# A down projection in seven products: sums of weight quarters kept in T, product order, and adds on POOL

## The chip, the cores and the metric

The kernel runs on one core of one Trainium2 chip. The core's engines work side by side: TensorE (PE in the profile, its weight loads PEld), VectorE (DVE), ScalarE (ACT), GpSimd (POOL) and SyncE (SP), which here only starts transfers. Each has its own instruction queue and meets the others through semaphores; transfers run on 16 DMA engines that all queues share. The metric is the device time of one execution in microseconds (us), as the median of several runs.

## The reference

One decoder layer on 512 tokens of width 1024, all in float32: two mixers (a state-space scan and a forgetting attention) with their projections, then a gated MLP with a causal convolution. The change touches the last matrix product of the MLP alone:

```
h = x @ w_up; h = causal_depthwise_conv(h, conv_w, conv_b)
gate, val = jnp.split(h, 2, axis=-1)
return (jax.nn.silu(gate) * val) @ w_down        # (512 x 2816) @ (2816 x 1024)
x = x + conv_gated_mlp(hf, ...)
```

## The kernel before, in words

**Precision.** TensorE takes operands in a shortened float format (fp32r). Each float32 operand is therefore split into a high part (a cast, on ScalarE) and a low part (the rest, a subtraction on VectorE), and each product is three matmuls: high by high, high by low, low by high (`mm3`, lines 110 to 112). For a weight unit that is `split_unit` (lines 726 and 727), for a left operand `split_into` (lines 756 and 757).

**Seven products.** The hidden activations (512 tokens by 2816) are cut in two token halves and two halves of the inner dimension, the weights w_down in two inner halves and two column halves: B11, B12, B21, B22. The block product is made in Strassen's manner with seven products of quarters in place of eight (Winograd's form): sums of activation quarters (`S1` to `S4`, and `a11`, `a12`, `a22`) by sums of weight quarters. The activation sums are made while the up projection runs (`sums`, lines 778 to 787, on POOL). The weight sums are made in the seven products, in the tiles T.

**A product.** A weight quarter is six units: five of two blocks of 128 x 512 (512 KB) and one of one block (256 KB). For each unit a product splits it into `wh` and `wl`, and runs 12 matmuls per block, two token blocks of 128 by three passes by two; in all 66 matmuls of 512 columns for the 11 blocks. Of `wh` and `wl` there are three buffers each, which the units use in turn; a unit's split can start when TensorE is done with the unit three back. The last two units of a product are taken together, sorted by token block. The result in PSUM (tiles X, Y, Z) is added to or subtracted from the residual tile `x2` on VectorE (line 874), and a finished block is stored (line 876). Products that share a result accumulate in one PSUM tile: Y in three of them, Z in two.

**Where the weights come from.** A plain quarter is loaded into a staging buffer `wraw` (`load_unit`, line 715; five buffers, SP's queue) and split from there. A sum is made in T: `fresh` (line 806) loads a quarter into T on SP's queue, and `gather` (line 809) adds another one by an accumulating transfer, on POOL's queue. T is a running sum. `next_sum(n, u)` is called after unit u of product n has been split; it may then be overwritten, with the sum that a later product wants. Before the change:

| product | left by weights | weights from | after its split, T becomes |
|---|---|---|---|
| 0 | a11 by B11 | wraw (three units split ahead, in `ready`) | B11 loaded, B12 accumulated |
| 1 | a12 by B21 | wraw | |
| 2 | S1 by T = B11 + B12 | T | B22 accumulated |
| 3 | S2 by T = B11 + B12 + B22 | T | B21 accumulated |
| 4 | a22 by T = all four | T | B22 loaded, B12 accumulated |
| 5 | S3 by T = B22 + B12 | T | |
| 6 | S4 by B22 | wraw | |

**Memory.** T's pool is opened after the up projection's pool (`pu`) is closed and takes its place in SBUF; a T tile may be written when the tiles that lay on its bytes are done with.

**Order.** The text gives every instruction's dependences and its place in program order. A planner (the tile framework's, line 950) sets the order of the instructions of each engine when the kernel is built: it moves ahead what it reckons to be ready. On the chip each queue then runs strictly in that order. So the left operand's split for a product three places on runs as soon as the buffer of a finished product's left operand is free, that is, where products meet.

Of the kernel before, what the change touches and what calls it, by code (L numbers as in the profile page):

```python
# [55 lines left out]
def tile_hybrid_layer(  # L56
# [20 lines left out]
    act, dve, pool, pe = nc.scalar, nc.vector, nc.gpsimd, nc.tensor  # L77
# [10 lines left out]
    def raw(ap):  # L88
        return ap.bitcast(F32)
# [18 lines left out]
    def mm3(o, ah, al, bh, bl, start, stop, grouped=True):  # L108
        kw = {} if grouped else {"skip_group_check": True}
        pe.matmul(o, ah, bh, start=start, stop=False, **kw)  # L110
        pe.matmul(o, ah, bl, start=False, stop=False, **kw)  # L111
        pe.matmul(o, al, bh, start=False, stop=stop, **kw)  # L112

    def bank(name="g"):
        return pg.tile([P, 512], F32, tag="g", name=name)

    def mbank(name="m"):
        return pm.tile([P, 512], F32, tag="m", name=name)
# [574 lines left out]
    def operand(slot=None):  # L693
        if slot is None:
            hl_ = [pb.tile([P, NH, HT], F32R, tag=t, name=t, bufs=2) for t in ("oh", "ol")]
            return hl_[0], hl_[1]
        pair_ = [pxt.tile([P, NK, SEQ], F32R, tag=t, name="o" + t) for t in ("xh", "xl")]
        return tuple(
            t.rearrange("p a b -> p (a b)")[:, 0 : NH * HT].rearrange("p (a b) -> p a b", b=HT) for t in pair_
        )  # L700
# [3 lines left out]
    S1, S2, S3, S4 = [pb.tile([P, NH, HT], F32, tag="S%d" % n, name="sum%d" % n) for n in (1, 2, 3, 4)]  # L704
    r2 = pb.tile([P, NTB], F32, tag="r2", name="r2")
    ss = pb.tile([P, NTB], F32, tag="ss", name="ss")
    UNITS = [(k, min(k + 2, NH)) for k in range(0, NH, 2)]
    B11, B12, B21, B22 = 0, 1, 2, 3

    def part(q, u):  # L710
        return wdown[q, :, UNITS[u][0] * 512 : UNITS[u][1] * 512]

    def load_unit(q, u):
        rw = wp.tile([P, 1024], F32, tag="wraw", name="wraw", bufs=5)
        nc.sync.dma_start(rw[:, 0 : (UNITS[u][1] - UNITS[u][0]) * 512], part(q, u))
        return rw
# [3 lines left out]
    def split_unit(u, src):  # L720
        n = (UNITS[u][1] - UNITS[u][0]) * 512
        where = pb if turn[0] % 3 == 2 else wp
        turn[0] += 1
        h = where.tile([P, 1024], F32R, tag="wh", name="wh")
        l = where.tile([P, 1024], F32R, tag="wl", name="wl")
        act.copy(h[:, :n], src[:, :n])  # L726
        dve.tensor_tensor(out=l[:, :n], in0=src[:, :n], in1=raw(h[:, :n]), op=ALU.subtract)  # L727
        return h, l
# [26 lines left out]
    def split_into(o, src, lo, hi):  # L755
        act.copy(o[0][:, lo:hi, :], src[:, lo:hi, :])
        dve.tensor_sub(o[1][:, lo:hi, :], src[:, lo:hi, :], raw(o[0][:, lo:hi, :]))
# [40 lines left out]
    ready = [split_unit(u, load_unit(B11, u)) for u in range(3)]  # L798
# [4 lines left out]
    T = [pt_.tile([P, 512 * (b - a)], F32, tag="T%d" % a, name="T%d" % a) for a, b in UNITS]  # L803

    def fresh(q, u):
        nc.sync.dma_start(T[u], part(q, u))

    def gather(q, u):
        nc.gpsimd.dma_start(T[u], part(q, u), accum_op=ALU.add)

    Y, Z, X1, X2 = (
        [mbank("Y") for _ in range(2)], [mbank("Z") for _ in range(2)], [bank("X") for _ in range(2)], None
    )
    ADD, SUB = ALU.add, ALU.subtract
    PRODUCTS = (
        (B11, None, Y, True, ((0, 0, ADD, False),)),
        (B21, None, X1, True, ((0, 0, ADD, True),)),
        (None, S1, Z, True, ((2, 512, ADD, False),)),
        (None, S2, Y, False, ((0, 512, SUB, False),)),
        (None, a22, X2, True, ((2, 0, ADD, False),)),  # L820
        (None, S3, Y, False, ((2, 0, ADD, True), (2, 512, SUB, True))),
        (B22, S4, Z, False, ((0, 512, ADD, True),)),
    )

    def next_sum(n, u):
        if n == 0:
            fresh(B11, u)
            gather(B12, u)
        elif n in (2, 3):
            gather(B22 if n == 2 else B21, u)  # L830
        elif n == 4:
            fresh(B22, u)
            gather(B12, u)

    ops = [a11, a12]
    for n, (quarter, _, tiles, start, adds) in enumerate(PRODUCTS):
        nxt = PRODUCTS[n + 1][1] if n + 1 < len(PRODUCTS) else None
        if nxt is not None:
            ops.append(operand(1 if n % 3 == 1 else None))
        tiles = [bank("X") for _ in range(2)] if tiles is None else tiles  # L840
        lhs = ops[n]
        final = n == len(PRODUCTS) - 1
        held = []
        for u, (lo, hi) in enumerate(UNITS):
            if n == 0 and u < len(ready):
                h, l = ready[u]
            else:
                h, l = split_unit(u, T[u] if quarter is None else load_unit(quarter, u))
            next_sum(n, u)
            if nxt is not None and u in (1, 2, 3):  # L850
                split_into(ops[n + 1], nxt, 4 * (u - 1), min(4 * u, NH))
            held.append((lo, hi, h, l))
            if u == len(UNITS) - 2:
                continue
            todo = [(k, i, b) for b in held for k in range(b[0], b[1]) for i in range(2)]
            held = []
            if u == len(UNITS) - 1:
                todo.sort(key=lambda t: t[1])
            for k, i, (lo_, _, h_, l_) in todo:
                c = slice((k - lo_) * 512, (k - lo_ + 1) * 512)  # L860
                s = slice(i * P, (i + 1) * P)
                mm3(
                    tiles[i], lhs[0][:, k, s], lhs[1][:, k, s], h_[:, c], l_[:, c], start and k == 0, k == NH - 1,
                    grouped=False,
                )
                if k == NH - 1:
                    for row, col, op, done in adds:
                        tb = row + i
                        cuts = 2 if final and i == 1 else 1
                        w = 512 // cuts  # L870
                        for cut in range(cuts):
                            c = slice(cut * w, (cut + 1) * w)
                            oc = slice(col + cut * w, col + (cut + 1) * w)
                            dve.tensor_tensor(out=x2[:, tb, oc], in0=x2[:, tb, oc], in1=tiles[i][:, c], op=op)
                            if done:
                                nc.sync.dma_start(out[tb * P : (tb + 1) * P, oc], x2[:, tb, oc])
# [77 lines left out]
```

## Time and profile before

| | |
|---|---|
| median of three runs | 845.64 us (845.4 to 849.22) |
| the profiled execution's own time | 845.59 us |
| its span in the trace | 843.8 us |
| TensorE matmuls, busy | 810.0 us (96%), 4590 |
| VectorE, ScalarE, POOL, busy | 630.9, 434.6, 291.4 us |
| plain transfers (q1) | 89.31 MB, 32.3% of 16 DMA engines |
| accumulating transfers (q0) | 11.54 MB, 7.0% |
| mean granted TensorE clock | 0.998 |

How to read it: a line such as `L727 DVE TENSOR_TENSOR wl<-T,wh 128x1024 ... x20` is a group of instructions: line of the kernel, engine, operation, output and inputs by their names in the program (buffer numbers left out), shape, count. "Idle before" is how long the engine stood before them, and the arrow names what ended that. A row of a timeline starts with the start and the duration in us. A row of stretches has, after its bounds and length, each engine's busy time with its instructions in the order PE, PEld, DVE, ACT, POOL, then the granted clock, the DMA engines' busy share and GB/s. A row of DMA queues has packets, MB and the time of its packets as a share of 16 engines over the window. A row of waits reads: who waited, for whom, us in total, times, longest.

### The profile page before, as it was taken

The page shows a single profiled execution, that of the slowest core. Times are in us where ns is not written, and L with a number is a line of the kernel's source. Part 1 is how long each engine was busy: PE and PEld are TensorE (multiplying, and loading weights), DVE is VectorE, ACT ScalarE, POOL GpSimd, SP SyncE. Part 2 cuts the span into 40 slices and gives each one's busy share as a digit, 9 for nine tenths or more (in the row PEclk, how much of TensorE's full clock was granted, in tenths as well). Part 3 has the DMA queues.
Part 4 walks back from the last instruction along what each step waited for, and adds up shares of the span by engine and source line. Part 5 has one row for each costly group of instructions (what it writes and reads, how often), then busy time and mean ns, then how long its engine had stood idle before and what let it go on. Part 6 is the DMA issues. An engine that isn't in the chain of part 4 may idle for free.

```text
span 843.8 us, 12403 instructions
## 1 busy us (share of the span) xinstructions
PE 810.0 (96%) x4590; PEld 696.6 (83%) x4590; DVE 630.9 (75%) x999; ACT 434.6 (52%) x830; POOL 291.4 (35%) x281
## 2 busy tenths in 40 slices
PE   6999989899989999999999999999999999998987
PEld 4888879779989898798898888888888888875766
DVE  7696998775779788997988767666666667875644
ACT  5456546443567675684575364444444444654432
POOL 3125253375445445135133413333333331332210
PEclk9999999999999999999999999999999999999999
DMA  8424322431442332333331222322222333599972
GB/s 313 164 76 130 100 101 76 133 105 50 140 123 86 104 101 92 96 112 107 95 101 51 95 81 100 99 99 89 91 97 100 100 100 109 160 304 240 241 169 88
DMA packets 32285, 101.63 MB, mean 120 GB/s; under 512 B 4129, under 2 KB 4961, under 8 KB 32225
## 3 DMA queue, kind: packets, MB, share of 16 engines
q1 hardware_dynamic: 28768, 89.31, 32.3%
q0 software_dynamic: 3456, 11.54, 7.0%
q8 instruction: 36, 0.59, 0.3%
q14 instruction: 25, 0.20, 0.1%
HBM read 94.44 MB, written 2.20 MB: 115 GB/s over the span
## 4 chain that ended last, share of the span: by engine, by line
PE 67%; DVE 13%; issue 7%; DMA 6%; POOL 3%; ACT 3%; SPq 0%; DVEq 0%; POOLq 0%; ACTq 0%
PE up L112 9%; PE up L110 9%; PE up L111 9%; DMA T<-in_wdown_dram 4%; PE pq L111 4%; PE pq L112 4%; PE pq L110 4%; PE po L112 3%; PE po L111 3%; PE po L110 3%; DVE xs L351 2%; PE o L580 1%; PE pT L566 1%; POOL ms L122 1%; PE Y L111 1%
## 5 line engine op out<-in xcount | busy, mean ns | idle before, releaser
L104 ACT CAST wh<-wraw 128x1024 fp32r<-128x1024 f32 x103 | 108.4, 1053 | 135.5 <-PE up L111 72.1
L110 PE MATMUL pq<-wh,xh 128*128 128x256 f32 x512 | 146.3, 288 | 0.0
L112 PE MATMUL pq<-wh,xl 128*128 128x256 f32 x512 | 146.2, 286 | 0.0
L111 PE MATMUL pq<-wl,xh 128*128 128x256 f32 x512 | 145.3, 284 | 0.6 <-DVE wl L105 0.6
L112 PE MATMUL up<-hh,wl 128*128 128x512 f32 (+1 forms) x368 | 140.2, 381 | 0.2 <-DVE wl L105 0.2
L111 PE MATMUL up<-hl,wh 128*128 128x512 f32 (+1 forms) x368 | 139.9, 380 | 0.0
L110 PE MATMUL up<-hh,wh 128*128 128x512 f32 (+1 forms) x368 | 139.8, 380 | 0.0
L105 POOL TENSOR_TENSOR wl<-wraw,wh 128x1024 fp32r<-128x1024 f32 x31 | 75.3, 2427 | 107.7 <-ACT wh L104 98.6
L105 DVE TENSOR_TENSOR wl<-wraw,wh 128x1024 fp32r<-128x1024 f32 x72 | 90.3, 1254 | 20.0 <-ACT wh L104 19.9
L111 PEld LDWEIGHTS pq<-wl,xh 128*128 128x128 f32 x512 | 97.8, 191 | 2.1 <-DVE wl L105 1.1
L110 PEld LDWEIGHTS pq<-wh,xh 128*128 128x128 f32 x512 | 97.5, 191 | 1.9 <-issue 1.2
L112 PEld LDWEIGHTS pq<-wh,xl 128*128 128x128 f32 x512 | 97.8, 191 | 0.7 <-issue 0.5
L112 PEld LDWEIGHTS up<-hh,wl 128*128 128x128 f32 x368 | 69.2, 188 | 13.8 <-DVE wl L105 0.4
L111 PEld LDWEIGHTS up<-hl,wh 128*128 128x128 f32 x368 | 69.2, 188 | 13.1
L110 PEld LDWEIGHTS up<-hh,wh 128*128 128x128 f32 x368 | 69.1, 188 | 13.1 <-issue 0.2
L765 DVE TENSOR_TENSOR up<-up,R 128x512 f32<-128x512 f32 x44 | 30.3, 691 | 57.0 <-PE up L112 57.0
L770 DVE SCALAR_TENSOR_TENSOR ua<-up,pc,ua 128x511 f32<-128x511 f32 (+1 forms) x88 | 67.1, 765 | 3.2 <-ACT ua L768 1.7
L526 POOL TENSOR_SCALAR bias<-cum,tokS 128x256 f32<-128x256 f32 (+1 forms) x32 | 22.4, 711 | 88.9 <-DVE nm L541 88.9
L254 DVE TENSOR_TENSOR x<-po,x 128x512 f32<-128x512 f32 x64 | 43.2, 683 | 10.1 <-PE po L112 9.5
L545 ACT ACTIVATE prob<-prob,nm 128x128 f32<-128x128 f32 (+1 forms) x64 | 35.9, 562 | 27.2 <-DVE nm L541 26.9
L780 POOL TENSOR_TENSOR ua<-ua 128x512 f32<-128x512 f32 x11 | 15.0, 1364 | 93.0 <-DVE ua L770 93.0
L727 DVE TENSOR_TENSOR wl<-T,wh 128x1024 fp32r<-128x1024 f32 (+1 forms) x24 | 26.9, 1134 | 26.2 <-ACT wh L726 26.2
(249 smaller groups left out, 1876.9 us busy)
## 6 DMA issues: line engine op xcount, KB each, us to landing
wraw<-in_wup_dram SPq DMA_DIRECT2D x44, 512.0 KB, 3.3
wraw<-in_wqkv_dram SPq DMA_DIRECT2D x24, 512.0 KB, 3.3
T<-in_wdown_dram POOLq DMA_DIRECT2D x20, 512.0 KB, 11.9
wraw<-in_wout_dram SPq DMA_DIRECT2D x16, 512.0 KB, 3.4
wraw<-in_wdown_dram SPq DMA_DIRECT2D x15, 512.0 KB, 4.6
wraw<-in_wxbc_dram SPq DMA_DIRECT2D x11, 512.0 KB, 4.0
T<-in_wdown_dram SPq DMA_DIRECT2D x10, 512.0 KB, 8.0
wraw<-in_wz_dram SPq DMA_DIRECT2D x8, 512.0 KB, 3.4
```

What stands on the lines that cost most here:

```text
L104: act.copy(h, r)
L105: (sub or dve).tensor_tensor(out=l, in0=r, in1=raw(h), op=ALU.subtract)
L110: pe.matmul(o, ah, bh, start=start, stop=False, **kw)
L111: pe.matmul(o, ah, bl, start=False, stop=False, **kw)
L112: pe.matmul(o, al, bh, start=False, stop=stop, **kw)
L254: dve.tensor_add(dst, o, dst)
L351: dve.scalar_tensor_tensor(out=dst[:, s:], in0=xp[:, : SEQ - s], scalar=half_w[:, cw + 3 - s : cw + 4 - s], in1=dst[:, s:], op0=ALU.mult, ...
L526: (dve if qb == 2 else pool).tensor_scalar(out=b, in0=cum[:, :n], scalar1=-1.0, scalar2=edge, op0=ALU.mult, op1=ALU.add)
L545: act.activation(p, p, AF.Exp, scale=-1.0, bias=nm[:, qb : qb + 1], accum_out=sm[:, qb : qb + 1])
L727: dve.tensor_tensor(out=l[:, :n], in0=src[:, :n], in1=raw(h[:, :n]), op=ALU.subtract)
L765: dve.tensor_mul(xp, o, R2)
L770: dve.scalar_tensor_tensor(out=a[:, s:], in0=xp[:, : SEQ - s], scalar=pc[:, cw + 2 - s : cw + 3 - s], in1=a[:, s:], op0=ALU.mult, op1=ALU.add,
```

## The change

Three things.

1. **Plain quarters go into T and are split there.** In product 0, units 3 to 5 of B11 are loaded into T (`source`) and split from T, instead of being loaded twice, into `wraw` for the product and into T for the sum. Units 0 to 2 are split ahead from `wraw` as before and loaded once more into T. After product 4, T gets B22 alone; the next product splits it from T.
2. **The last two products change places.** S4 by B22 is now product 5, with T = B22; after its split B12 is accumulated on it, and S3 by T = B22 + B12 is the last product. That one has two destinations, both token blocks by both column halves, where the last one before had one.
3. **Two units of each of three sums are added on POOL.** For the sums after products 0 (units 1 and 3), 2 and 3 (units 1 and 4), the quarter's unit is loaded into a `wraw` buffer on SP's queue, and POOL adds it to T by an instruction, in place of an accumulating transfer.

The number of matmuls, of splits and of left operands stays the same.

```
         (None, a22, X2, True, ((2, 0, ADD, False),)),
+        (None, S4, Z, False, ((0, 512, ADD, True),)),
         (None, S3, Y, False, ((2, 0, ADD, True), (2, 512, SUB, True))),
-        (B22, S4, Z, False, ((0, 512, ADD, True),)),
     )
+    ADDED = {0: B12, 2: B22, 3: B21, 5: B12}
+    BY_POOL = {0: (1, 3), 2: (1, 4), 3: (1, 4)}
 
     def next_sum(n, u):
+        if n == 0 and u < len(ready):
+            fresh(B11, u)
+        if n == 4:
+            fresh(B22, u)
+        elif u in BY_POOL.get(n, ()):
+            w = (UNITS[u][1] - UNITS[u][0]) * 512
+            pool.tensor_tensor(out=T[u][:, :w], in0=T[u][:, :w], in1=load_unit(ADDED[n], u)[:, :w], op=ADD)
+        elif n in ADDED:
+            gather(ADDED[n], u)
+
+    def source(n, u):
+        quarter = PRODUCTS[n][0]
         if n == 0:
-            fresh(B11, u)
-            gather(B12, u)
-        elif n in (2, 3):
-            gather(B22 if n == 2 else B21, u)
-        elif n == 4:
-            fresh(B22, u)
-            gather(B12, u)
+            fresh(quarter, u)
+        return T[u] if n == 0 or quarter is None else load_unit(quarter, u)
...
-                h, l = split_unit(u, T[u] if quarter is None else load_unit(quarter, u))
+                h, l = split_unit(u, source(n, u))
             next_sum(n, u)
```

More of the change, by code (lines that the diff above doesn't have):

```diff
@@ L820, in tile_hybrid_layer @@
         (None, a22, X2, True, ((2, 0, ADD, False),)),
+        (None, S4, Z, False, ((0, 512, ADD, True),)),
         (None, S3, Y, False, ((2, 0, ADD, True), (2, 512, SUB, True))),
-        (B22, S4, Z, False, ((0, 512, ADD, True),)),
     )
+    ADDED = {0: B12, 2: B22, 3: B21, 5: B12}
+    BY_POOL = {0: (1, 3), 2: (1, 4), 3: (1, 4)}
     def next_sum(n, u):
-        if n == 0:
-            fresh(B11, u)
-            gather(B12, u)
-        elif n in (2, 3):
-            gather(B22 if n == 2 else B21, u)
-        elif n == 4:
-            fresh(B22, u)
-            gather(B12, u)
+        if n == 0 and u < len(ready):
[9 more added lines that the diff above has]
+        quarter = PRODUCTS[n][0]
+        if n == 0:
+            fresh(quarter, u)
+        return T[u] if n == 0 or quarter is None else load_unit(quarter, u)
     ops = [a11, a12]
-    for n, (quarter, _, tiles, start, adds) in enumerate(PRODUCTS):
+    for n, (_, _, tiles, start, adds) in enumerate(PRODUCTS):
         nxt = PRODUCTS[n + 1][1] if n + 1 < len(PRODUCTS) else None
```

## The prediction

> **What bounds the kernel now.** I read the page first: its span, its lane of slices, its DMA lane.
>
> ```profile
> span 843.8 us, 12403 instructions
> ...
> PE   6999989899989999999999999999999999998987
> ...
> PEclk9999999999999999999999999999999999999999
> DMA  8424322431442332333331222322222333599972
> ```
>
> TensorE is nearly full and its clock is whole everywhere; the DMA engines are full only in slices 36 to 39, which is the down projection. The change touches nothing earlier, so I cut that stage at the first matmul of each of its seven products (call them P0 to P6), from the timeline of TensorE, and then took the busy times of the stretches between.
>
> ```profile
> 722.52 0.61 PE L110 MATMUL Y<-wh,oh 128*128 128x512 f32 x2
> ...
> 737.60 0.63 PE L110 MATMUL X<-wh,oh 128*128 128x512 f32 x2
> ...
> 753.37 0.63 PE L110 MATMUL Z<-wh,oxh 128*128 128x512 f32 x2
> ...
> 771.18 0.50 PE L110 MATMUL Y<-wh,oh 128*128 128x512 f32 x1 [0.59 <-ACT wh L726]
> ...
> 789.18 0.40 PE L110 MATMUL X<-wh,oh 128*128 128x512 f32 x1
> ...
> 806.41 0.50 PE L110 MATMUL Y<-wh,oxh 128*128 128x512 f32 x1 [1.30 <-ACT wh L726]
> ...
> 823.76 0.40 PE L110 MATMUL Z<-wh,oh 128*128 128x512 f32 x1
> ...
> 839.01 0.40 PE L112 MATMUL Z<-wh,ol 128*128 128x512 f32 x1
> ```
>
> ```profile
> 722.50:737.60 15.10, 15.10 (x67) 12.39 (x66) 12.37 (x13) 9.71 (x12) 5.54 (x4) 1.00 0.59 167
> 737.60:753.40 15.80, 15.41 (x68) 12.34 (x67) 10.92 (x12) 7.91 (x10) 5.91 (x7) 1.00 1.04 315
> 753.40:771.20 17.80, 16.29 (x68) 11.89 (x66) 9.60 (x11) 7.86 (x9) 4.53 (x6) 1.00 1.07 268
> 771.20:789.20 18.00, 16.04 (x67) 12.19 (x68) 12.34 (x13) 9.36 (x11) 5.15 (x6) 1.00 1.07 213
> 789.20:806.40 17.20, 15.53 (x67) 12.11 (x65) 9.49 (x11) 7.33 (x9) 3.40 (x4) 1.00 1.01 262
> 806.40:823.80 17.40, 16.24 (x67) 12.22 (x68) 9.43 (x10) 6.85 (x7) 1.74 (x2) 1.00 0.66 137
> 823.80:839.40 15.60, 15.57 (x67) 12.09 (x65) 7.92 (x10) 3.83 (x5) 0.00 (x0) 1.00 0.21 79
> ```
>
> Every product has the same 66 matmuls. P0 takes 15.08 us (737.60 less 722.52), P1 15.77, but P2 17.81, P3 18.01, P4 17.23, P5 17.35. In P1 to P4 the DMA share (last but one number) is 1.0 or more. The table of waits and the groups of instructions say for what:
>
> ```profile
> POOL T L809 <- DMA T<-in_wdown_dram: 37.3, 12, 11.4
> ```
>
> ```profile
> L726 ACT CAST wh<-T 128x1024 fp32r<-128x1024 f32 x20 | 20.9, 1048 | 34.5 <-DMA T<-in_wdown_dram 27.5 <-PE Y L112 5.4 <-DVE wl L727 1.4
> ```
>
> POOL, before it accumulates, waits for the plain load, and ScalarE's split of a sum tile T waits for the accumulating DMA that makes it, and TensorE stands behind the split. So the stage is bound by TensorE, with DMA lateness on top in P2 to P5.
>
> **The change, part by part.** First the price of a transfer, from two DMA stretches: 772 to 790 us, accumulating transfers practically alone; 733 to 747 us, mostly plain ones.
>
> ```profile
> q0 software_dynamic: 1100, 3.76, 106.0%
> ```
>
> ```profile
> q1 hardware_dynamic: 1244, 4.10, 82.6%
> ```
>
> 3.76 MB in 18 us is 209 GB/s, so an accumulated unit of 512 KB costs 2.5 us of all DMA engines; 4.10 MB in 0.826 x 14 = 11.6 us is 355 GB/s, 1.5 us for a plain one. A quarter is five units and a half one. The change takes away the second load of B22 (5.5 units, 8.2 us) and of the last three units of B11 (2.5 units, 3.7 us), and turns six accumulating units plain (6 us): 18 us less of DMA in a stage whose DMA is full for some 70 us.
>
> *Term 1, lateness of the sums.* Per product afterwards: P2 and P3 carry 3.5 x 2.5 + 2 x 1.5 = 11.8 us of transfers, P4 only the 8.2 us of a plain B22, P5 13.8 us of accumulation. All are under the 15.1 us that the matmuls take, where P4 before had 8.2 + 13.8 = 22 us between the split and the next use. The swap gives each half of that its own product. I therefore let P2, P3 and P4 fall to P1's 15.77 (P1's sums are not late) and P5 to 15.28, the mean of P0 and P6: 2.04 + 2.24 + 1.46 + 2.07 = 7.8 us gained. Bounds: nothing (if DMA stays late) and 9.4 us (if all four fall to 15.08, P0's, which would also remove the stall of the next paragraph). I take 7.8.
>
> *Term 2, the adds on POOL.* P1's extra 0.7 us is a stall that every product from P1 to P4 has. Here is VectorE at the start of P2:
>
> ```profile
> 754.32 1.22 DVE L727 TENSOR_TENSOR wl<-T,wh 128x1024 fp32r<-128x1024 f32 x1
> 755.45 3.22 DVE L757 TENSOR_TENSOR ol<-a,oh 128x1024 fp32r<-128x1024 f32 x3
> 758.59 1.22 DVE L727 TENSOR_TENSOR wl<-T,wh 128x1024 fp32r<-128x1024 f32 x1
> ```
>
> ```profile
> 759.87 0.50 PE L111 MATMUL Z<-wl,oxh 128*128 128x512 f32 x1 [0.39 <-DVE wl L727]
> ```
>
> Unit 1 is split, then a chain of three operand splits (L757) runs, and only then unit 2, for which TensorE already waits. So at this place there is no slack. In P2 and P3 the new POOL add of unit 1 is released by exactly that split of unit 1 (it overwrites the T that the split reads), so it falls into the chain. What POOL and VectorE do to each other when both read two SBUF tiles:
>
> ```profile
> 278.88 3.42 DVE L468 TENSOR_TENSOR tok<-tok,ms 128x1024 f32<-128x1024 f32 x1 [2.80 <-POOL ms L122]
> ```
>
> ```profile
> 278.82 2.40 POOL L105 TENSOR_TENSOR wl<-wraw,wh 128x1024 fp32r<-128x1024 f32 x1
> ```
>
> ```profile
> 664.12 1.61 POOL L787 TENSOR_TENSOR sum<-ua,sum 128x256 f32<-128x256 f32 x1
> ```
>
> ```profile
> 663.74 1.38 DVE L105 TENSOR_TENSOR wl<-wraw,wh 128x1024 fp32r<-128x1024 f32 x1 [0.17 <-ACT wh L104]
> 665.04 0.96 DVE L783 TENSOR_TENSOR ol<-ua,oh 128x256 fp32r<-128x256 f32 x1
> ```
>
> The first pair: VectorE started 0.06 us after POOL and ended 1.08 us after POOL's end; it stood still meanwhile. The second: POOL stood until VectorE's first instruction ended, then went ahead of the second one, although that followed at once. So an add of 2.40 us, of the size the change issues, gets in after the first link of the chain and shifts the rest and the split of unit 2 by about 2.35 us; with no slack TensorE loses that twice, 4.7 us. Bounds: 0 (VectorE keeps its turn, or the chain lies elsewhere) and 7.1 (P0's add too). I take 4.7, because the second pair shows who goes next. The adds of units 3 and 4 come in mid-product: a unit's split may start when TensorE frees its buffers three units back, so it has two units of 15.1 / 5.5 = 2.74 us for a cast and a subtraction (1.05 + 1.22), 3.2 us of slack against 2.35; I cost them at nothing. On POOL's queue the accumulation of unit 2 stands behind the add of unit 1, but it waits for the later split of unit 2 anyhow; and the six quarters' units that move to SP's queue go to staging buffers that nothing else wants after P1, so they are there early.
>
> The Trainium skill, "SBUF — State Buffer", section "Who interferes with whom", has this as a rule against the change: a VectorE instruction with two SBUF inputs and a GpSimd one that reads SBUF lock each other out for the whole instruction, and who issues first decides. The trace agrees on the lock (3.42 us above). By the rule alone a chain whose links follow without a gap could keep POOL out to its end, and term 2 would then lie anywhere from nothing to 4.7.
>
> *Term 3, the end.* Before, three additions and three stores follow the last matmul:
>
> ```profile
> 838.99 1.35 DVE L874 TENSOR_TENSOR x<-x,Z 128x512 f32<-128x512 f32 x3 [5.08 <-PE Z L112]
> ```
>
> ```profile
> 839.70 1.30 SPq L876 DMA_DIRECT2D out_dram<-x  x3
> ```
>
> The swapped last product has two destinations, so six additions and six stores. Additions: double, 1.35 more. Stores: SP issues one each 0.43 us, 1.3 more, all behind the first addition, and they carry 1.05 MB, at 355 GB/s 3.0 us, 0.4 more than the 2.6 us over which six issues spread. I take 1.6 lost (1.3 to 1.9).
>
> *Term 4, the start.* Units 3 to 5 of B11 now load into T instead of the staging buffers, and T lies in memory that the pool of the up projection gives back.
>
> ```profile
> 732.40 0.33 SPq L715 DMA_DIRECT2D wraw<-in_wdown_dram  x1
> 732.79 4.36 SPq L806 DMA_DIRECT2D T<-in_wdown_dram  x6
> ```
>
> ```profile
> 733.94 1.50 POOL L787 TENSOR_TENSOR sum<-ua,sum 128x256 f32<-128x256 f32 x1
> ```
>
> ```profile
> SPq L806 <- POOL sum L787: 0.3, 1, 0.3
> ```
>
> ```profile
> 724.72 2.35 DVE L757 TENSOR_TENSOR oxl<-sum,oxh 128x1024 fp32r<-128x1024 f32 x2
> ```
>
> One T load waited for POOL's last sum, done at 735.44, while TensorE is through the three units split in advance at 722.52 + 3 x 2.74 = 730.7. If it then waited for unit 3 (fourth load, some 734.3, cast 1.05 us) it would lose 8.7 us, with a landing as for staged loads in the stretch before:
>
> ```profile
> wraw<-in_wdown_dram SPq DMA_DIRECT2D x8, 512.0 KB, 4.1
> ```
>
> But the planner moves ready work forward: the T loads, written in P0, were issued behind B21's loads of P1, and the first operand split, written in P1, ran at 724.72 in P0. B21's staged units can fill the hole and P0's rest come after. Cost between 0 and 8.7; I take 0, as nothing but program order would hold TensorE. The two staging buffers that wait for POOL's adds leave B21 three of five; a buffer cycle of 4.1 + 2.3 us over three is 2.1 us a unit, under 2.74: nothing.
>
> **Sum.** -7.8 + 4.7 + 1.6 + 0 = -1.5 us. The profiled run took 845.59 us by its own time (span 843.8 and 1.8 around it), the median is 845.64: so 844.1.
>
> **Rivals.** (A) *The adds hide.* Term 2 is zero: 845.6 - 7.8 + 1.6 = 839.4, or 841 with one partial collision. For it: the order of the chain is the planner's and may come out otherwise. Against: nothing in the change touches the order of the splits there. (B) *P0 waits for T.* Slower than before: the mechanism is term 4, at units 3 to 5 of P0; 844.1 + 8.7 = 852.8 in full, 850 where B21 fills part. It decides from a stall of 5.8 us on. Against: the moved work above. (C) *The sums stay late*, since T goes through the same chain of load, add, split, and the last accumulation now stands before the last product, with 13.8 us of transfers for 15.1: half of term 1, 848. For it: accumulations land late (T waits of up to 11.4 us above). Against: 18 us of DMA less.
>
> **Chances.** Forecast 0.44, A 0.26, B 0.16, C 0.14. A measurement of this kernel tells about 0.5% (4.2 us) from no change: under 841.4 is faster, over 849.8 slower. A and the low edge of the forecast give faster 0.30; B and a little of C slower 0.20; the rest, 0.50, no change. The range reaches from A's 839.4 to 850.5, which cuts off B's worst and A's luckiest. The forecast's own range, no change, is 841.5 to 847.5.
>
> **What would show it.** Term 1: P2 to P5 each shorter, hardly any wait of ScalarE for T. Term 2: in P2 and P3 an operand split of some 3.4 us under a POOL add, and TensorE idle some 2.7 us before unit 2. Term 3: six additions from the last matmul on and the end 1.6 us further from it. Term 4: whether X matmuls of P1 stand before the last units of P0. I am wrong if P0 holds a long idle of TensorE, or if unit 2 isn't late.

## The result, and the profile after

The changed kernel takes 856.0 us (median of four runs, 853.2 to 858.1) beside 846.15 us for the kernel before in the same comparison: a ratio of 1.011, 95% interval 1.0084 to 1.0134. It is slower by about 9 us, where 844.1 was predicted, with 850.5 as the upper end. The profiled execution took 854.63 us, of which the span is 852.8.

First the page of the kernel after: its span, TensorE's busy lane, the lane of its granted clock and the DMA lane, in forty slices of 21.3 us.

```profile
span 852.8 us, 12395 instructions
...
PE   8999989899989999999999999999999999798997
...
PEclk9999999999999999999999999999999999899999
DMA  8423332421532332243322223222232333875583
```

The last six slices are the down projection. Their DMA digits have fallen from 599972 to 875583; over the whole kernel the plain and the accumulating queue moved 88.26 and 8.39 MB, 4.2 MB less than before, as the prediction counted (8 units of 512 KB). But TensorE has a 7 in slice 35 where it had a 9, and the clock lane has an 8, which it had nowhere before. The stretches between the first matmuls of the seven products say which product that is (columns as before: bounds and length, busy time of PE, PEld, DVE, ACT, POOL with instructions, granted clock, DMA share, GB/s).

```profile
724.00:747.93 23.93, 18.28 (x68) 14.00 (x67) 12.24 (x13) 9.82 (x13) 12.62 (x10) 0.86 0.83 244
747.93:763.53 15.60, 15.32 (x68) 12.32 (x67) 10.75 (x12) 8.25 (x10) 0.86 (x1) 1.00 0.64 183
763.53:781.50 17.97, 15.38 (x68) 12.32 (x67) 14.37 (x12) 8.29 (x10) 9.15 (x6) 1.00 0.68 132
781.50:801.07 19.57, 16.98 (x68) 13.43 (x67) 13.49 (x12) 8.28 (x10) 8.29 (x5) 0.91 0.60 98
801.07:816.84 15.77, 15.39 (x68) 12.31 (x67) 10.89 (x12) 8.34 (x10) 0.85 (x1) 1.00 0.53 179
816.84:831.97 15.13, 15.13 (x68) 12.38 (x67) 7.92 (x9) 5.87 (x7) 4.26 (x5) 1.00 0.99 173
831.97:847.10 15.13, 15.13 (x67) 12.20 (x65) 6.70 (x8) 3.87 (x5) 0.00 (x0) 1.00 0.20 54
```

Against before, P0 is longer by 8.84 us (23.92 against 15.08) and P3 by 1.57. P4 and P5 are shorter by 1.46 and 2.22; P1, P2 and P6 together by 0.36. The stretch from the last matmul's start to the end grew by 1.14. P0 begins 1.49 us later, with nothing changed in the text ahead of it; it differs from run to run (721.4 to 729.0 in the traces of the experiments). 8.84 + 1.57 - 1.46 - 2.22 - 0.36 + 1.14 + 1.49 = 9.0 us, which is the difference of the spans.

**P0.** The timelines of TensorE, ScalarE, VectorE, SP's queue and POOL, and a row of the chain that ended last (start, duration, what), all of the kernel after, around the place where unit 3 should begin:

```profile
731.98 0.40 PE L112 MATMUL Y<-wh,ol 128*128 128x512 f32 x1
737.80 1.22 PE L110 MATMUL Y<-wh,oh 128*128 128x512 f32 x2 [5.42 <-ACT wh L726]
739.25 0.79 PE L111 MATMUL Y<-wl,oh 128*128 128x512 f32 x1 [0.23 <-DVE wl L727]
...
744.23 0.40 PE L111 MATMUL Y<-wl,oh 128*128 128x512 f32 x1
...
747.93 0.62 PE L110 MATMUL X<-wh,oh 128*128 128x512 f32 x2
```

```profile
736.70 1.04 ACT L726 CAST wh<-T 128x1024 fp32r<-128x1024 f32 x1 [3.56 <-DMA T<-in_wdown_dram]
740.90 1.05 ACT L726 CAST wh<-T 128x1024 fp32r<-128x1024 f32 x1 [3.15 <-DMA T<-in_wdown_dram]
744.07 0.62 ACT L726 CAST wh<-T 128x512 fp32r<-128x512 f32 x1 [2.13 <-DMA T<-in_wdown_dram]
```

```profile
737.78 1.41 DVE L727 TENSOR_TENSOR wl<-T,wh 128x1024 fp32r<-128x1024 f32 x1 [3.65 <-ACT wh L726]
```

```profile
734.74 0.81 SPq L806 DMA_DIRECT2D T<-in_wdown_dram  x2
```

```profile
729.51 7.11 DMA T<-in_wdown_dram
```

```profile
733.22 1.49 POOL L787 TENSOR_TENSOR sum<-ua,sum 128x256 f32<-128x256 f32 x1
```

After the three units split in advance TensorE has nothing: unit 3's cast waits for its load into T. That load is the fourth on SP's queue, behind T0 to T2 that nobody wants yet. It is issued at 729.51 and lands 7.11 us later, at 736.6, where the prediction took 4.1 us. Units 4 and 5 cannot even be issued before POOL's last sum (L787) has left the memory that they take, at 734.7. No matmul of P1 stands in the gap; the first is at 747.93. So rival B, given 0.16, is what happened.

**P2 and P3.** VectorE's rows where the new add of unit 1 meets the chain of operand splits in P2, then POOL's row, then TensorE's:

```profile
765.61 5.43 DVE L757 TENSOR_TENSOR ol<-a,oh 128x1024 fp32r<-128x1024 f32 x3
770.96 1.21 DVE L727 TENSOR_TENSOR wl<-T,wh 128x1024 fp32r<-128x1024 f32 x1
```

```profile
765.78 3.30 POOL L834 TENSOR_TENSOR T<-T,wraw 128x1024 f32<-128x1024 f32 x1 [2.71 <-DVE wl L727]
```

```profile
772.23 0.51 PE L111 MATMUL Z<-wl,oxh 128*128 128x512 f32 x1 [2.59 <-DVE wl L727]
```

The three splits that took 3.22 us before now take 5.43; taken singly, the second of them, from 766.74 on, takes 3.42. TensorE waits 2.59 us for the split of unit 2, where it waited 0.39. This is the collision that the prediction described. P3 has the same rows (the chain 5.43 at 783.57, TensorE's wait 2.59 at 790.19) but is 1.6 us longer than P2.

**The clock.** P3's surplus, and a part of P0's, shows in the last but two column of the stretches above: a granted clock of 0.86 in P0 and of 0.91 in P3. Cut finer, the stretches of the kernel after show that the clock is whole or half:

```profile
733.59:737.00 3.41, 0.00 (x0) 0.00 (x0) 0.55 (x1) 0.30 (x1) 3.41 (x3) 1.00 0.58 141
737.00:740.42 3.42, 2.39 (x5) 1.48 (x6) 1.41 (x1) 0.75 (x1) 3.06 (x3) 0.50 1.01 265
740.42:743.83 3.41, 3.41 (x10) 2.64 (x9) 1.22 (x1) 1.05 (x1) 1.31 (x2) 0.50 1.05 271
743.83:747.24 3.41, 3.41 (x16) 2.74 (x15) 1.92 (x2) 1.85 (x3) 1.63 (x2) 1.00 1.06 300
767.72:771.14 3.42, 1.92 (x9) 1.25 (x7) 3.42 (x3) 1.53 (x2) 1.36 (x1) 1.00 0.23 84
771.14:774.55 3.41, 2.32 (x10) 1.93 (x11) 3.30 (x3) 0.00 (x0) 1.74 (x3) 1.00 0.19 16
788.20:791.62 3.42, 1.43 (x6) 1.20 (x7) 3.42 (x4) 0.07 (x1) 0.87 (x1) 1.00 0.00 0
791.62:795.03 3.41, 3.41 (x10) 2.62 (x9) 1.46 (x2) 0.62 (x1) 3.26 (x2) 0.50 0.89 138
```

From 737.00 on TensorE ran 6.83 us at half clock (10 matmuls in a full window, 16 when whole). Of the 8.84 us of P0, 5.6 are standing still (737.80 less 731.98 less one matmul's 0.23). Another 1.0 goes to the low part of unit 3: it was done at 739.19, and the two matmuls ahead of it need 0.45 at whole clock. The remaining 2.25 fall behind that, mostly at half clock. But the clock is not the whole reason for them: unit 4 was late too (its cast waited until 740.90 for the load), with its low part done at 743.20, and the first matmul that needs it ran at 744.23. With a whole clock it could have run 1.0 us earlier at most, so of P0's loss at most 1.0 us is the clock's, and the late loads of units 3 to 5 are the rest. In P3 nothing else was late, and 3.41 us at half clock cost 1.6 to 1.7 us.

### The profile page after: what moved, and what is told of

It is laid out like the page before. It is cut to its first block, busy times and chain, and to the rows that moved or that the text cites. A ratio compares the mean times of both kernels' runs of the same rounds, so it can differ in the third digit from the quotient of the medians.

```text
span 852.8 us, 12395 instructions
## 1 busy us (share of the span) xinstructions
PE 815.0 (96%) x4590; PEld 702.0 (82%) x4590; DVE 637.0 (75%) x1000; ACT 434.3 (51%) x830; POOL 301.2 (35%) x281
## 3 DMA queue, kind: packets, MB, share of 16 engines
q1 hardware_dynamic: 28480, 88.26, 31.9%
q0 software_dynamic: 2592, 8.39, 5.6%
## 4 chain that ended last, share of the span: by engine, by line
PE 69%; DVE 14%; issue 7%; POOL 3%; DMA 3%; ACT 2%; SPq 0%; DVEq 0%; POOLq 0%; ACTq 0%
PE up L110 9%; PE up L112 9%; PE up L111 9%; PE pq L111 4%; PE pq L112 4%; PE pq L110 4%; PE po L112 3%; PE po L111 3%; PE po L110 3%; DVE xs L351 2%; PE Y L111 1%; PE o L580 1%; PE Y L112 1%; POOL ms L122 1%; PE pT L566 1%
## 5 line engine op out<-in xcount | busy, mean ns | idle before, releaser
L727 DVE TENSOR_TENSOR wl<-T,wh 128x1024 fp32r<-128x1024 f32 (+1 forms) x33 | 38.3, 1181 | 30.1 <-ACT wh L726 30.1
L726 ACT CAST wh<-T 128x1024 fp32r<-128x1024 f32 (+1 forms) x33 | 31.7, 970 | 55.8 <-PE Z L112 18.8
```

## The experiments

The theory after the result: (a) P0's loss is its wait for late T loads, and nothing but the order of the text holds TensorE there; (b) the adds on POOL cost P2 and P3 the collision; (c) term 1 of the prediction was gained in full and is hidden under the two. The rivals were that the adds and their staging loads make the T loads late, that the sums of P2 and P3 are late by themselves, and that the adds buy something by taking work off the DMA engines.

**B11 staged again.** The changed kernel, with units 3 to 5 of B11 loaded into `wraw` for the product and again into T, as before the change.

```
-        if n == 0 and u < len(ready):
+        if n == 0:
             fresh(B11, u)
...
-        if n == 0:
-            fresh(quarter, u)
-        return T[u] if n == 0 or quarter is None else load_unit(quarter, u)
+        return T[u] if quarter is None else load_unit(quarter, u)
```

> Undoes one of the three parts in P0 alone: units 3 to 5 of B11 are split from staging buffers again and loaded a second time into T. Theory (P0 waits for T loads that queue behind T's first three units and behind the up projection's memory): P0 falls from 23.9 us back to about 15.1, the half-clock stretch of 6.8 us in P0 goes with the idle, P2 and P3 keep their 2.75 us idle before unit 2; total 856.0 - 8.8 = 847.2. Rival (the DMA traffic saved there is what keeps the sums in time): P0 gets short, but P2 and P3 grow again by lateness of T, some 2 us each; 851.

Measured: 853.31 us, ratio 1.0068 (1.0044 to 1.0092). P0's gap is gone, P0 takes 15.08 us. But P1 takes 22.46. VectorE's and POOL's rows at P1's start:

```profile
739.42 5.41 DVE L757 TENSOR_TENSOR ol<-sum,oh 128x1024 fp32r<-128x1024 f32 x3
744.75 3.53 DVE L727 TENSOR_TENSOR wl<-wraw,wh 128x1024 fp32r<-128x1024 f32 x1
```

```profile
740.60 3.42 POOL L834 TENSOR_TENSOR T<-T,wraw 128x1024 f32<-128x1024 f32 x1
...
744.57 2.62 POOL L834 TENSOR_TENSOR T<-T,wraw 128x1024 f32<-128x1024 f32 x1
```

With P0 on time, the two adds that follow P0 fall into P1's chain of operand splits: one is issued while its second link runs and gets in ahead of the third (taken singly, the links start at 739.42, 740.56 and 741.69, and the third takes 3.14), the other gets in ahead of the split for which TensorE waits. TensorE stands 5.27 us there (743.06 to 748.34, start to start) and then runs 6.83 us at half clock. So the expectation failed, by a collision that P0's own gap had covered in the changed kernel.

**The adds of P2 and P3 moved to unit 0**, ahead of the chain instead of into it:

```
-    BY_POOL = {0: (1, 3), 2: (1, 4), 3: (1, 4)}
+    BY_POOL = {0: (1, 3), 2: (0, 4), 3: (0, 4)}
```

> The changed kernel with POOL's adds after P2 and P3 on units 0 and 4 instead of 1 and 4; nothing else. Theory (the add of unit 1 locks VectorE out inside the chain of operand splits): unit 0's add falls on the residual additions, which read one SBUF input only; the 2.75 us idle before unit 2 in P2 and P3 falls to the 0.55 us that P1 and P4 have, an operand split there takes 1.22 us instead of 3.42; 4.4 us less, up to 6 where the half-clock stretch in P3 goes too: 850 to 851.6. Rival (TensorE waits there for the chain and the transfers, not for the lock): no change, 856.

Measured: 848.62 us, ratio 1.0016 (0.9989 to 1.0042). P2 and P3 take 15.76 and 15.77 us, and VectorE's chain of P2 is back at its old length:

```profile
771.05 3.22 DVE L757 TENSOR_TENSOR ol<-a,oh 128x1024 fp32r<-128x1024 f32 x3
```

P0 keeps its gap (24.38 us). So in P2 and P3 the whole loss, 6.0 us, was the place of the add, half clock included. The median fell by 7.4 us, more than the 4.4 to 6 expected; the profiled execution, 854.01 us, is the slowest of the ten, so no trace shows where the other 1.4 were gained.

**Both edits together.**

```
-    BY_POOL = {0: (1, 3), 2: (1, 4), 3: (1, 4)}
+    BY_POOL = {0: (1, 3), 2: (0, 4), 3: (0, 4)}
...
-        if n == 0 and u < len(ready):
+        if n == 0:
...
-        return T[u] if n == 0 or quarter is None else load_unit(quarter, u)
+        return T[u] if quarter is None else load_unit(quarter, u)
```

> Both edits together. If they are separate causes they add up: 856.0 - 8.8 - 4.4 to 6 = 841.2 to 842.8, that is 0.4 to 0.6% under the kernel before. If the saved traffic of B11 carried the gain of P2 to P5, P2 to P5 are late again: 846 or more.

Measured: 848.04 us, ratio 1.0018 (0.9996 to 1.0040): a miss, for the same reason as in the first experiment. P1 takes 22.55 us with the same gap of 5.27, and P2 still 16.67; P3 to P5 are 15.74, 15.78 and 15.13. In P2 the add of unit 0 runs from 759.62 to 762.02 here, beside unit 1's split, which takes 2.13 us instead of 1.22, and TensorE waits 1.26 us for unit 2.

**Staged, and no adds at all.** What is left of the change is T = B22 loaded once and split there, and the swap.

```
-    BY_POOL = {0: (1, 3), 2: (1, 4), 3: (1, 4)}
+    BY_POOL = {}
...
-        if n == 0 and u < len(ready):
+        if n == 0:
...
-        return T[u] if n == 0 or quarter is None else load_unit(quarter, u)
+        return T[u] if quarter is None else load_unit(quarter, u)
```

> B11 staged in P0 as in the kernel before, and no add on POOL: all sums by accumulating transfers; what is left of the change is that T = B22 is split directly and that the last two products are swapped. Theory A (the swap and the 8.2 us of B22 saved are enough: 13.8 us of accumulation per product under 15): P2 and P3 take 15.8 us, total 842. Theory B (the adds are what brings the sums in time): P2 and P3 stay at 17.5 to 18 by T's lateness, P4 and P5 are short, total 846.

Measured: 839.4 us, ratio 0.9908 (0.9876 to 0.9940): faster than both kernels. Its stretches, P2 to P5:

```profile
754.24:770.02 15.78, 15.40 (x67) 12.31 (x66) 10.89 (x12) 8.29 (x10) 5.62 (x7) 1.00 1.07 225
770.02:785.79 15.77, 15.39 (x67) 12.31 (x66) 10.89 (x12) 8.30 (x10) 4.26 (x5) 1.00 1.06 208
785.79:801.56 15.77, 15.39 (x67) 12.31 (x66) 10.89 (x12) 8.30 (x10) 0.85 (x1) 1.00 0.72 221
801.56:816.69 15.13, 15.13 (x67) 12.38 (x66) 7.92 (x9) 5.86 (x7) 4.29 (x5) 1.00 0.97 172
```

P2 to P5 fall from 17.81, 18.00, 17.23 and 17.35 to 15.78, 15.77, 15.77 and 15.13: 7.94 us, with every sum made by accumulating transfers. The DMA share in P2 and P3 is 1.07, as high as before (1.07 in both). A full DMA lane there isn't a late one; the adds, meant to empty it, had nothing to gain.

**No adds, but B11's units in T.** The changed kernel with `BY_POOL = {}` alone.

```
-    BY_POOL = {0: (1, 3), 2: (1, 4), 3: (1, 4)}
+    BY_POOL = {}
```

> The changed kernel with no add on POOL: all sums by accumulating transfers; B11's units 3 to 5 still in T, the products still swapped. Theory (P0 waits for its late T loads, whoever makes the sums): P0 about 24 us with one stall of 5 to 6 us and a half clock behind it, P1 to P6 as in e6_staged_no_pool (15.1 to 15.8 each), so 839.4 + 8.8 = 848 us. Rival (the adds on POOL or the staging loads for them delay the T loads): P0 15 to 18 us, 839 to 842 us.

Measured: 848.75 us, ratio 1.0017 (0.9994 to 1.0039). P0 takes 23.94 us, in the changed kernel 23.92, and the same row ends its gap:

```profile
735.29 1.22 PE L110 MATMUL Y<-wh,oh 128*128 128x512 f32 x2 [5.49 <-ACT wh L726]
```

So the adds and their staging loads have no part in P0's gap. The two kernels without adds differ in B11 alone: 1.1 in a hundred by the ratios, some 9 us, and 8.86 in P0's length. The ratio is also that of the kernel with the adds at unit 0 (1.0016): placed there, and with P0 late, the adds neither cost nor gain anything.

**The T loads earlier.** The kernel of the last experiment, with the tiles of units 3 to 5 placed on memory that comes free first and their loads first on SP's queue.

```
-    T = [pt_.tile([P, 512 * (b - a)], F32, tag="T%d" % a, name="T%d" % a) for a, b in UNITS]
+    T = [None] * len(UNITS)
+    for u in (3, 4, 5, 0, 1, 2):
+        a, b = UNITS[u]
+        T[u] = pt_.tile([P, 512 * (b - a)], F32, tag="T%d" % a, name="T%d" % a)
...
+    for u in (3, 4, 5, 0, 1, 2):
+        fresh(B11, u)
```

(The two calls of `fresh(B11, u)` inside the products are taken out.)

> As e5_no_pool_adds, but the T tiles of units 3 to 5 lie where the up projection's tiles are given back first, and their loads are issued first on SP's queue. Theory (the T loads are late because they are issued late, behind tiles that are still in use and behind the loads of T0 to T2): P0's stall falls to 2 us or less, no half clock, 840 to 843 us. Rival (the landing itself takes too long, 5 to 7 us after the issue however early the queue comes to it): P0 stays at 20 us or more, 845 to 848 us.

Measured: 846.25 us, ratio 0.9984 (0.9961 to 1.0007); the profiled execution took 842.07. In that one P0 is 18.41 us: the gap before unit 3 has shrunk to 1.77 us, with a second of 1.0 us behind it, and no half clock follows. The second line below is from the view of the six T loads, issued from 725.3 to 733.3:

```profile
732.70 0.72 PE L110 MATMUL Y<-wh,oh 128*128 128x512 f32 x2 [1.77 <-ACT wh L726]
```

```profile
DMA to landing us min/median/max: 3.7/6.9/7.3
```

Early issue gives back 5.5 of the 8.9 us of P0. What is left of the stall goes with the landing, 6.9 us in the middle where the prediction took the 4.1 of staged loads. Seven of the ten runs took 845.4 us or more, with no trace of their own; where these lost the 4 us more isn't known. The theory's "840 to 843" holds for the profiled run, not for the median.

**B21 in between.** Again the kernel without adds, with the first three units of P1 written between units 0 to 2 and units 3 to 5 of P0.

```
-    for n, (_, _, tiles, start, adds) in enumerate(PRODUCTS):
+    for n, us in ((0, (0, 1, 2)), (1, (0, 1, 2)), (0, (3, 4, 5)), (1, (3, 4, 5))) + tuple(
+        (n, range(6)) for n in range(2, 7)
+    ):
...
-        for u, (lo, hi) in enumerate(UNITS):
+        for u in us:
```

> As e5_no_pool_adds (B11's units 3 to 5 in T, no adds on POOL), but the text itself does what the prediction took the planner to do: the first three units of P1 (B21, staged) stand between units 0 to 2 and units 3 to 5 of P0, so TensorE has 8.2 us of other work while the T loads land. Theory (only the order of the text held TensorE in P0): no stall over 1 us, no half clock, P0 and P1 together 31 us (39.6 in e5_no_pool_adds), 840 us. Rival (the T loads or the splits behind them are too late even for that, or B21's units wait for staging buffers): a stall of 3 us or more remains and the time is 844 us or more.

Measured: 840.74 us, ratio 0.9917 (0.9892 to 0.9943). P0 and P1 together take 31.52 us against 39.57 without this edit (23.94 + 15.63), and their clock is whole:

```profile
722.21:753.73 31.52, 30.77 (x133) 24.62 (x132) 23.55 (x24) 18.00 (x21) 10.61 (x10) 1.00 0.82 209
```

TensorE goes from P0's third unit straight to P1, and waits 0.22 us and then 0.53 us where it comes back to P0:

```profile
730.42 0.63 PE L110 MATMUL X<-wh,oh 128*128 128x512 f32 x2
...
739.05 0.73 PE L110 MATMUL Y<-wh,oh 128*128 128x512 f32 x2 [0.22 <-ACT wh L726]
```

This is the decisive one for the failed step. The T loads could be late, as B21 could fill the hole; the order of the matmuls on TensorE's queue had to say so. Without this edit the planner left that order as the text has it. It does not always: in this same trace two matmuls of P2 (752.81) stand before the last four of P1. Why it left a hole of 5.6 us open isn't shown.

**B22 late, nothing else.** From the kernel before: B22 for the last product goes into T after product 5's split, in place of `wraw`, where it had been loaded far ahead. No swap, no adds.

```
-        (B22, S4, Z, False, ((0, 512, ADD, True),)),
+        (None, S4, Z, False, ((0, 512, ADD, True),)),
...
         elif n == 4:
             fresh(B22, u)
             gather(B12, u)
+        elif n == 5:
+            fresh(B22, u)
```

> The kernel before with one difference: B22 for the last product is not loaded into a staging buffer but into T, after product 5 has split it; order of the products, sums and B11 as before. Theory 1 (the sums of P2 to P4 were late because the early second load of B22 into the staging buffers competed with them): P2, P3 and P4 fall to 15.8 us, P5 stays near 17.3 as its T carries a plain load and an accumulation, P6 near 15.1 to 16: 846 - 2.0 - 2.2 - 1.5 = 840 to 841 us. Theory 2 (the accumulating transfers are late by themselves, and it was the swap that took the load off): P2 to P5 stay at 17 to 18 us, 846 us.

Measured: 843.84 us, ratio 0.9954 (0.9932 to 0.9976). P2, P3 and P4 fall to 15.77 us each, and P5 rises to 20.01:

```profile
784.65:800.42 15.77, 15.39 (x68) 12.31 (x67) 9.98 (x11) 7.37 (x9) 2.56 (x3) 1.00 0.89 228
800.42:820.43 20.01, 17.36 (x68) 11.76 (x66) 8.92 (x10) 6.71 (x7) 2.59 (x3) 1.00 0.99 274
```

So the lateness of P2 to P4 (5.7 us) was one thing alone: the second load of B22, early, ahead of what the sums needed. P5's was another: a plain load and an accumulation between two uses, and it is gone in every kernel with the swap. Here it grows to 4.9 us over the 15.13 of the swapped kernels. That P4 no longer runs late and so leaves the transfers less time, or that B22's loads for the last product now fall into P5 (DMA share 0.99, before 0.66): no run separates the two. (The expectation had P5 stay near 17.3: a miss of 2.7 us.)

**The adds alone**, on the kernel before:

```
-            gather(B12, u)
-        elif n in (2, 3):
-            gather(B22 if n == 2 else B21, u)
+        if u in BY_POOL.get(n, ()):
+            pool.tensor_tensor(out=T[u], in0=T[u], in1=load_unit(ADDED[n], u), op=ADD)
+        elif n in ADDED:
+            gather(ADDED[n], u)
```

> The kernel before with the adds on POOL alone (after P0 units 1 and 3, after P2 and P3 units 1 and 4). Theory (an add on POOL locks VectorE out where the operand splits stand): P1 has a stall of 4 to 5 us and a half clock behind it (about 22 us), P2 and P3 are 18 to 19.6 us each, P4 less late than before as fewer accumulations stand before it: 846 + 6.7 + 1 = 851 to 855 us. Rival (the adds take transfers away from a stage that is short of them and are worth that): P2 to P4 fall to 16, 841 to 843 us.

Measured: 855.34 us, ratio 1.0096 (1.0065 to 1.0127). P1 takes 23.00 us; VectorE's chain there:

```profile
743.11 7.57 DVE L757 TENSOR_TENSOR ol<-sum,oh 128x1024 fp32r<-128x1024 f32 x3
```

Two adds meet it, 3.22 + 2 x 2.2 us. P2 to P6 are 17.95, 19.57, 15.76, 16.25 and 15.48. The adds do relieve P4 and P5 (1.47 and 1.10 us), and cost P1 and P3 8.8. P2's 17.95 is as long as before (17.81), with the collision in place of the late sums.

**Two queues for the last stores.** The fastest kernel so far, with the stores of the right-hand columns on ScalarE's queue.

```
-                                nc.sync.dma_start(out[tb * P : (tb + 1) * P, oc], x2[:, tb, oc])
+                                q = nc.scalar if final and col else nc.sync
+                                q.dma_start(out[tb * P : (tb + 1) * P, oc], x2[:, tb, oc])
```

> As e6_staged_no_pool, with the final stores of the right-hand columns issued on ScalarE's queue, those of the left-hand columns on SyncE's. Theory (the six stores are issued one behind the other on one queue, and that is what the longer tail is): the stretch from the last matmul's start to the end falls from 6.3 to 5.3 to 5.7 us, 838.5 to 839 us. Rival (the tail is the landing of the last store's bytes): 6.2 us as before, 839.4 us. The times are too close for the medians; the trace decides.

Measured: 839.43 us, ratio 0.9897 (0.9865 to 0.9929); the stretch from the last matmul's start to the end is 6.23 us against 6.26. The last store is issued earlier after the first addition (2.7 us instead of 3.25) but lands no sooner (5.2 us after it in both). So the issue isn't what makes the tail longer; the landings follow each other at the same distance (0.4 to 0.7 us in both) whichever queue they come from.

The lengths of all seven products, from one first matmul to the next (us):

| kernel | ratio | P0 | P1 | P2 | P3 | P4 | P5 | P6 |
|---|---|---|---|---|---|---|---|---|
| before | 1 | 15.08 | 15.77 | 17.81 | 18.00 | 17.23 | 17.35 | 15.48 |
| after | 1.0109 | 23.92 | 15.60 | 17.97 | 19.57 | 15.77 | 15.13 | 15.13 |
| B11 staged | 1.0068 | 15.08 | 22.46 | 17.96 | 19.56 | 15.76 | 15.13 | 15.13 |
| adds at unit 0 | 1.0016 | 24.38 | 15.60 | 15.76 | 15.77 | 15.77 | 15.13 | 15.13 |
| both of these | 1.0018 | 15.08 | 22.55 | 16.67 | 15.74 | 15.78 | 15.13 | 15.13 |
| staged, no adds | 0.9908 | 15.08 | 15.74 | 15.78 | 15.77 | 15.77 | 15.13 | 15.13 |
| in T, no adds | 1.0017 | 23.94 | 15.63 | 15.79 | 15.77 | 15.77 | 15.13 | 15.13 |
| T loads earlier | 0.9984 | 18.41 | 15.62 | 15.77 | 15.77 | 15.77 | 15.13 | 15.13 |
| B22 late alone | 0.9954 | 15.08 | 15.76 | 15.77 | 15.77 | 15.77 | 20.01 | 15.48 |
| adds alone | 1.0096 | 15.08 | 23.00 | 17.95 | 19.57 | 15.76 | 16.25 | 15.48 |

## Why the prediction was wrong, point by point

**Term 4 is the step that failed**: "Cost between 0 and 8.7; I take 0, as nothing but program order would hold TensorE." It measured 8.84. The overlap with B21 that was to make it 0 did not take place: program order did hold TensorE, and the kernel with B21 between is the proof. The reason given for 0 was that the planner had moved two other things forward, B21's loads ahead of the T loads, and an operand split. Neither was a matmul. In the trace of before, TensorE's rows have all 66 of a product ahead of the next one's first at every boundary, also where the next product's sums were late; the prediction quoted the first of each and didn't draw the conclusion. The bound's working missed as well. It had unit 3's load issued 11.7 us after P0's start (734.3, as before the change), landing 4.1 us later, and so a stall of 8.7 us. The load was issued after 5.5 us and took 7.1 us, and the stall was 5.6 us. That the measured 8.84 lies so near 8.7 is luck: what makes up the difference is the low part of unit 3, the lateness of units 4 and 5, and at most 1.0 us of half clock, of which the bound had none.

**Term 2**, 4.7 us for the adds: the mechanism is shown, place and size. The chain grew by 2.21 us in P2 and in P3 (5.43 against 3.22); against the kernel without adds the two products lost 2.19 and 3.80, together 6.0. The surplus is P3's half clock. By the Trainium skill, "SBUF — State Buffer", section "Who interferes with whom", the one that issues first decides. Here POOL's add stood from 765.78, during the first link, and got in ahead of the second, which followed at 766.74 without a gap; so the reading that a chain keeps POOL out to its end is not what these rows show. P0's adds, costed at nothing, were free only because P0 stood still: they cost P1 6.7 us with P0 on time.

**Term 1**, 7.8 us: 7.94 in the kernel without adds. The cause was narrower than "18 us less of DMA": P2 to P4 needed only B22's early second load gone, and P5 needed the swap. In the changed kernel it shows in P4 and P5 (3.7 us), and is buried in P2 and P3.

**Term 3**, 1.6 us: 1.14 in the changed kernel, 1.4 without adds. That SP's issue would set it is refuted by the run with two queues; P6 gives 0.35 back. In the traces with six stores the stretch from the last matmul to the end lies between 5.96 and 6.43 us, so one trace tells its length to some 0.5.

Put together from its own terms with 8.84 for 0 and 6.0 for 4.7, the sum is -7.8 + 6.0 + 1.6 + 8.84 = 8.6 us, 854.2 for the profiled run, which took 854.63. So close a fit is in part luck too: it has too much for the end (1.14, less P6's 0.35) and nothing for P0's later begin (1.49).

## What to carry to other kernels

When an operand that stood ready is made to arrive later, the question isn't whether other work is ready but whether the engine's own order puts it there: read that order from the trace of before, at the boundary in question. A full DMA lane says nothing of lateness; find which transfer stands ahead of the late one, since here one early prefetch made three products wait and its removal was worth 5.7 us, and the work moved to POOL relieved two products of 2.6 and cost two others 8.8. A change of three parts is worth running part by part: the swap with B22's single load alone gained 0.9%. B11's units in T lost 1.1% (without adds, against staged), and the adds lost 1.6% (with B11 staged, against none).

## What the runs showed of the hardware

The half clock was not expected. The granted clock went to 0.50 in whole windows of 3.41 us, and in the down projection what decided was how much of the preceding window on that grid TensorE had stood still. An idle of 2.6 us in P3, 2.0 of it in one window, left TensorE busy 1.43 of 3.42 us (788.20 to 791.62), and the next window ran at half; the same idle in P2 lay across two windows, busy 1.92 and 2.32, and the clock stayed whole. The kernel with staged B11 and the one with the adds alone repeat this, half clock in P3 and none in P2. The nearest case from the other side is P2 with staged B11, where the window after this one was still whole:

```profile
766.64:770.06 3.42, 1.57 (x7) 1.31 (x8) 3.42 (x4) 0.00 (x0) 1.05 (x2) 1.00 0.00 0
```

Back from half takes more: in P0 a window busy 2.39 of 3.42 us was followed by another at half, and only a full one by a whole clock. The Trainium skill, "TensorE: Matmul & The Clock Gate", in Part 1 and in "HAM oscillation — how this bites in real kernels", has a window of 3413 ns that runs free, and the rule to have no idle gap over about 3.4 us. The window agrees with the 3.41 us here; the gap that sufficed was shorter, 2.6 us. Between a share of 42% and 46% of a window busy lies the point that these rows leave open. One window outside the down projection does not fit (the kernel with the adds at unit 0, 162.70 to 166.11, with matmuls of 64 columns among them: busy 2.04 of 3.41, half clock behind it), so the busy share is not shown to be the whole rule.
